# Output projection of a decoder layer: from a blocked product in 192 matmuls to Strassen's scheme in seven products

## The chip, the cores and the metric

The kernel runs on one core of a Trainium2 chip. The metric is the time of one execution on the device in microseconds (us). The kernel before was run three times: median 813.8 us, from 813.42 to 814.41. One further execution was taken by the hardware profiler; its own numbers stand in the table below.

## What is computed

One layer of a decoder on 512 tokens of width 1024, in float32. Two token mixers run in parallel: dilated window attention and a state-space scan. Each goes through its own projection (the branches), the two are merged by sigmoid gates, and the result is projected by `w_out`, added to the scaled input and normalized; a gated feed-forward part follows. What matters here is the middle:

```python
gates = jax.nn.sigmoid((gate_logits + b_gate[layer]).astype(jnp.float32))
mixed = gates[..., 0, :] * y_attn + gates[..., 1, :] * y_ssm
mix_out = mixed.astype(x.dtype) @ w_out[layer]            # (512 x 1024) @ (1024 x 1024)
h = layer_norm(DN_ALPHA * x + mix_out.astype(x.dtype), ln1_g[layer], ln1_b[layer])
ff = (jax.nn.silu(h @ w_ff_gate[layer]) * (h @ w_ff_up[layer])) @ w_ff_down[layer]
x = layer_norm(DN_ALPHA * h + ff.astype(h.dtype), ln2_g[layer], ln2_b[layer])
```

## The kernel before, in words

**Numbers in two parts.** Every float32 matrix that enters a matmul is split: `hi` is the value cast to the type fp32r (done by ACT, ScalarE), and `lo` is the rest, value minus `hi` (done by DVE, VectorE). A product is three matmuls, hi x hi, hi x lo and lo x hi (`mm3`, lines 205 to 208), all added up in one PSUM bank. In `add_remainder` (line 1509) the low part is made without DVE: ACT writes -hi into `lo`, and a transfer issued by POOL (GpSimd) adds the raw value from DRAM to it (line 1511). An adding transfer is a DMA with `accum_op=ALU.add`.

**Weights.** The class `Weights` hands out the weights in order. A unit of 1024 KB is loaded by SP (SyncE) into one of two `wraw` buffers and split in two halves into slots of hi and lo; `release()` gives back the oldest slot, and the next half is split into it at once. When the second half of a unit is split, `load()` issues the load of the unit after next. When the units are used up, functions listed in `w.jobs` and `w.loads` take their place: the feed-forward weights. `w.after` holds a postponed subtraction, which the next `flush()` emits. There are three slots at first and two more (`pb`) once the attention's tiles are freed (line 1429).

**Order of the work.** The schedule is written out by hand: on each engine the instructions run in the order of the program. A tile that takes the place of an older one waits until all uses of the older one are over. `home(n, ...)` names such a place of 8 KB per partition.

**Branches, lines 1394 to 1423.** Eight steps n = 0 to 7, each with 24 matmuls of 512 columns. From n = 4 on, the gated sums become the mixer's output `mx` (line 1416 hi, line 1421 lo), two of eight K-slices per step.

**Output projection, lines 1560 to 1636.** Four token tiles t of 128, two halves of 512 columns, eight K-slices, three matmuls each: 4 x 2 x 8 x 3 = 192 matmuls. The first half's four tiles are summed side by side while the units of `w_out` are split; the second half goes tile by tile. `wo_out` (line 1566) adds the scaled input from PSUM and takes the statistics of the normalization on DVE; `rstd` has one small operation on POOL; `normalize_shared` (line 1455) does half of a tile on DVE and half on ACT and POOL. `turn_h` (line 1573) transposes a normalized tile by eight PE transposes and splits it; `turn_lows` emits the subtractions on DVE.

**What stands around it.** The feed-forward product is already done by Strassen's scheme in pairs of blocks: `product(j, n)` is pair j, product n, 24 matmuls of 256 columns. Pair 0 needs sums of weight blocks: s5 from the block `early`, s6 and s3 and s7 from `early` and `ra[0]` (lines 1604, 1611, 1629, 1631). Its first products (0,1) and (0,2) use token tiles 0 and 1 only; tiles 2 and 3 are turned behind them. The weights (0,1), (0,2), (1,1), (1,2) are loaded by POOL as hi directly (line 1531), and their low parts come by adding transfers.

Of the kernel before, what the change touches and what calls it, by code (L numbers as in the profile page):

```python
# [16 lines left out]
P = 128  # L17
# [154 lines left out]
def emit(ctx, tc, i, out):  # L172
# [42 lines left out]
    def kslice(pair, k, cols=slice(None)):  # L215
        return pair[0][k // 4][:, k % 4, cols], pair[1][k // 4][:, k % 4, cols]
# [30 lines left out]
    w = Weights(nc, wp, split)  # L247
    out_homes = deque(("g0", 2, 6, 3))
    w.add(None, 8)
# [1142 lines left out]

    mx = act_pair("mix")
    for n in range(8):
        ws = w.views[N_BR + n]
        src = (gh_, gl_) if n < 4 else (merged["h"], merged["l"])
# [13 lines left out]
        for c, (ch, t0, t1) in enumerate(ts_):  # L1410
            if n < 4:
                stt(t1, t1, 1.0, bs[c], ALU.add, ALU.mult)
            else:
                stt(t0, t0, 1.0, bs[c], ALU.add, ALU.mult)
                tt(t0, t0, t1, ALU.add)
                act.mul(kslice(mx, ch)[0], t0, 0.5)
        flush()
        if n >= 4:
            for ch, t0, _ in ts_:
                hi, lo = kslice(mx, ch)  # L1420
                stt(lo, t0, 0.5, hi.bitcast(F32), ALU.mult, ALU.subtract)
        w.release()
# [46 lines left out]
    ht = []  # L1469
    early = home(7, "early")  # L1470
    sp.dma_start(early, i["w_gu"][1])
    s5 = home(8, "s5")[:, 0:1024]
    s6 = bt.tile([P, 1024], F32, tag="fth", name="s6", bufs=1)
# [25 lines left out]
    def load_dn(z, block, q):  # L1499
        dn[block, q] = z  # L1500
        sp.dma_start(z, i["w_dq"][block, q])

    w.loads[ff_first] = deque((lambda j=j: load_a(j)) for j in (0, 1))

# [21 lines left out]
    def prepare(j, n):  # L1526
# [9 lines left out]
        if j == 0 and n in (5, 6, 3, 7):  # L1536
            src = {5: s5, 6: s6, 3: s3, 7: s7}[n]
# [21 lines left out]

    def wo_mm(d, n, t):  # L1560
        ws = w.views[N_OUT + n]
        for k in range(2):
            kk = 2 * (n % 4) + k
            mm3(d, kslice(mx, kk, slice(128 * t, 128 * t + 128)), (ws[0][:, k, :], ws[1][:, k, :]), kk == 0, kk == KT - 1)

    def wo_out(d, t, e):
        cs = slice(512 * e, 512 * e + 512)
        stt(hn[t][:, cs], xn[t // 2][:, t % 2, cs], ALPHA, d, ALU.mult, ALU.add)
        dve.bn_stats(bst1[t][:, e, :], hn[t][:, cs])

    hturn = ring(4, 5, 6, 7)

# [21 lines left out]

    od = [bank(4 + t, f"wo0{t}") for t in range(NTT)]
    for n in range(4):
        for t in range(NTT):
            wo_mm(od[t], n, t)
        if n < 3:
            w.release()  # L1600
            if n < 2:
                w.split()
        if n == 2:
            tt(s5, early[:, 0:1024], early[:, 1024:2048], ALU.add)
    for t in range(NTT):
        wo_out(od[t], t, 0)
    od = [bank(t, f"wo1{t}") for t in range(NTT)]
    w.release()
    while w.free:
        w.split()  # L1610
    tt(s6, s5, ra[0][:, 0:1024], ALU.subtract)
    w.flush()
    mvs = [bt.tile([P, 4], F32, name=f"mva{t}", bufs=1) for t in range(NTT)]
    for t in range(NTT):
        for n in range(4, 8):
            wo_mm(od[t], n, t)
            if n == (None, None, 6, 5)[t]:
                turn_h(t - 2)
        if t == 3:
            turn_lows()  # L1620
            normalize_shared(hn[2], mvs[2], lnb)
        wo_out(od[t], t, 1)
        dve.bn_aggr(mvs[t][:, 0:2], bst1[t])
        rstd(mvs[t])
        turn_lows()
        if t < 2:
            normalize_shared(hn[t], mvs[t], lnb)
        if t == 0:
            tt(s3, ra[0][:, 1024:2048], s6, ALU.subtract)
        if t == 1:  # L1630
            tt(s7, ra[0][:, 0:1024], early[:, 0:1024], ALU.subtract)
            hp_ = tuple([home(h, f"h{n}{j}", F32R).rearrange("p (k t) -> p k t", k=4) for j, h in enumerate(hs)] for n, hs in (("h", (7, 8)), ("l", ("g1", 1))))
        if t in (0, 1):
            for _ in range(2):
                remainders.popleft()()
    normalize(hn[3], mvs[3], lnb)


# [10 lines left out]

    sums = home(6, "sums").rearrange("p (n c) -> p n c", n=2)  # L1650
    quad = home(3, "quad").rearrange("p (c e t) -> p c e t", c=4, e=2)
# [473 lines left out]
```

## Time and profile before

| | before |
|---|---|
| median of three runs | 813.8 us |
| profiled execution, its own time | 813.21 us |
| its span, first to last instruction | 811.4 us |
| mean granted TensorE clock | 0.995 |
| PE busy | 799.9 us (99%) |
| DVE busy | 669.8 us (83%) |
| ACT busy | 417.3 us (51%) |
| POOL busy | 88.5 us (11%) |
| DMA, all queues | 122.73 MB, mean 151 GB/s |

How to read the profile: times are microseconds from the span's start unless marked ns. PE is the matmul engine, PEld its weight loads; DVE is VectorE, ACT is ScalarE, POOL is GpSimd, SP is SyncE, which here only issues transfers. L1511 is line 1511 of the kernel. A line of a timeline gives start, duration, engine, line, operation, result <- operands, shape, how many were merged (x2), and in brackets how long the engine sat idle before and what it waited for. A group line gives minimum, median and maximum duration in ns, first and last start, and the shape. A waits line gives who waited for whom, the sum, the number of times and the longest. A windows line gives, for a stretch of time, the busy time and count of PE, PEld, DVE, ACT and POOL, then the granted clock, the busy share of the 16 DMA engines and GB/s moved. The chain of work that ended last is followed back from the last instruction.

### The profile page before, as it was taken

To read this page: it belongs to the slowest core of one execution; us is meant where nothing else is said; L and a number is where in the kernel's file an instruction comes from. 1 tells how busy PE (TensorE), PEld (TensorE's weight loads), DVE (VectorE), ACT (ScalarE), POOL (GpSimd) and SP (SyncE) were. 2 spreads that over 40 slices of the span, in tenths; PEclk is the share of its full clock that TensorE was granted. 3 is DMA by queue.
4 is the path that set the end of the run, shared out by engine and by line. 5 is a ranking of instruction groups with operands and counts; after the bars stand their busy time and mean duration, and the time that the engine had idled before them with its cause. 6 is when DMAs were issued, how large, how long until landed. Compare 5 with 4: busy or idle time off the path is not lost.

```text
span 811.4 us, 13836 instructions
## 1 busy us (share of the span) xinstructions
PE 799.9 (99%) x5584; PEld 720.1 (89%) x5584; DVE 669.8 (83%) x1066; ACT 417.3 (51%) x615; POOL 88.5 (11%) x110
## 2 busy tenths in 40 slices
PE   9999999999999999999999999999999999999995
PEld 7888888888999999988888899999999999888884
DVE  7987998979788799466796799887777789788986
ACT  5973222537575645874243466555555556554521
POOL 0000002230011333000000620000000000010105
PEclk9999999999999999999999999999999999999998
DMA  8753447895145654751728373622222324674544
GB/s 333 195 122 102 139 156 230 207 196 147 30 113 119 147 103 108 239 190 52 282 106 286 68 219 86 252 105 104 104 105 105 105 104 154 263 160 149 139 122 104
DMA packets 33488, 122.73 MB, mean 151 GB/s; under 512 B 7824, under 2 KB 12688, under 8 KB 23952
## 3 DMA queue, kind: packets, MB, share of 16 engines
q1 hardware_dynamic: 23808, 91.83, 33.0%
q0 software_dynamic: 7984, 28.32, 16.9%
q10 hardware_dynamic: 1632, 1.70, 0.6%
q8 instruction: 44, 0.72, 0.4%
q14 instruction: 20, 0.16, 0.1%
HBM read 105.84 MB, written 9.70 MB: 142 GB/s over the span
## 4 chain that ended last, share of the span: by engine, by line
PE 95%; DMA 2%; POOL 1%; DVE 1%; issue 0%; ACT 0%; DVEq 0%; POOLq 0%
PE qx L1261 7%; PE dnx L1872 6%; PE dnz L1872 4%; PE qz L1261 4%; PE pu L616 3%; PE pg L206 3%; PE vx L1217 3%; PE pg L207 3%; PE pg L208 3%; PE dny L1872 2%; DMA wlo<-in_w_gu 2%; PE s L840 2%; PE b L206 2%; PE b L207 2%; PE b L208 2%; PE qy L1261 2%
## 5 line engine op out<-in xcount | busy, mean ns | idle before, releaser
L1543 ACT CAST whi<-sums 128x1024 fp32r<-128x1024 f32 x40 | 42.0, 1051 | 61.3 <-DVE sums L344 61.3
L200 DVE TENSOR_TENSOR wlo<-raw,whi 128x1024 fp32r<-128x1024 f32 x40 | 48.8, 1223 | 16.4 <-ACT whi L199 16.4
L199 ACT CAST whi<-raw 128x1024 fp32r<-128x1024 f32 x40 | 41.7, 1048 | 17.1 <-PE pk L207 11.3
L344 DVE TENSOR_TENSOR wlo<-sums,whi 128x1024 fp32r<-128x1024 f32 x40 | 48.8, 1220 | 0.0
L1156 ACT CAST whi_q<-rq 128x1024 fp32r<-128x1024 f32 x28 | 29.3, 1052 | 35.7 <-DVE rq L344 25.1
L344 DVE TENSOR_TENSOR wlo_q<-rq,whi_q 128x1024 fp32r<-128x1024 f32 x28 | 34.2, 1221 | 15.8 <-ACT whi_q L1156 15.6
L1872 PE MATMUL dnx<-whi_d,pc 128*128 128x512 f32 (+1 forms) x128 | 38.2, 376 | 0.0
L853 ACT ACTIVATE un<-un,st 128x256 f32<-128x256 f32 (+1 forms) x64 | 30.9, 487 | 13.3 <-DVE st L851 13.3
L206 PE MATMUL pg<-x_hi,whi 128*128 128x512 f32 x96 | 37.6, 392 | 0.0
L778 POOL DMA_DIRECT2D kq<-qz x32 | 25.3, 1752 | 111.8 <-ACT un L865 70.9
L207 PE MATMUL pg<-x_lo,whi 128*128 128x512 f32 x96 | 37.4, 390 | 0.0
L208 PE MATMUL pg<-x_hi,wlo 128*128 128x512 f32 x96 | 37.4, 389 | 0.0
L968 ACT ACTIVATE gt<-pg,bgate 128x512 f32<-128x512 f32 x12 | 8.3, 690 | 41.8 <-PE pg L208 41.8
L1784 ACT CAST whi_d<-dn 128x1024 fp32r<-128x1024 f32 x16 | 16.9, 1056 | 23.0 <-DVE dn L344 11.1
L1872 PEld LDWEIGHTS dnx<-whi_d,pc 128*128 128x128 f32 x128 | 23.6, 188 | 4.4
L1794 POOL DMA_DIRECT2D whi_db<-in_w_dp x3 | 1.6, 547 | 228.8 <-PE dny L1872 225.1
L1872 PE MATMUL dnx<-wlo_d,pc 128*128 128x512 f32 (+1 forms) x64 | 24.1, 376 | 0.0
L1261 PE MATMUL qx<-x23h,whi_q 128*128 128x256 f32 x80 | 23.1, 289 | 0.0
L1261 PE MATMUL qz<-x_hi,whi_q 128*128 128x256 f32 x80 | 22.9, 287 | 0.0
L1261 PE MATMUL qz<-x_hi,wlo_q 128*128 128x256 f32 x80 | 22.6, 283 | 0.0
L1261 PE MATMUL qz<-x_lo,whi_q 128*128 128x256 f32 x80 | 22.6, 283 | 0.0
L1261 PE MATMUL qx<-x23h,wlo_q 128*128 128x256 f32 x80 | 22.6, 283 | 0.0
(894 smaller groups left out, 2627.9 us busy)
## 6 DMA issues: line engine op xcount, KB each, us to landing
raw<-in_w_in SPq DMA_DIRECT2D x12, 1024.0 KB, 5.4
ra<-in_w_gu SPq DMA_DIRECT2D x11, 1024.0 KB, 4.8
rb<-in_w_gu SPq DMA_DIRECT2D x10, 1024.0 KB, 4.9
rq<-in_w_quad SPq DMA_DIRECT2D x16, 512.0 KB, 4.4
dn<-in_w_dq SPq DMA_DIRECT2D x8, 1024.0 KB, 4.8
rv<-in_w_in SPq DMA_DIRECT2D x4, 1024.0 KB, 8.6
kq<-qz POOLq DMA_DIRECT2D x32, 128.0 KB, 5.9
raw<-in_w_br SPq DMA_DIRECT2D x4, 1024.0 KB, 5.0
```

Source lines behind the costliest of these rows:

```text
L199: act.copy(hi, src)
L200: dve.tensor_tensor(lo, src, hi.bitcast(F32), op=ALU.subtract)
L206: pe.matmul(dst, a[0], b[0], start=first, stop=False)
L207: pe.matmul(dst, a[0], b[1], start=False, stop=False)
L208: pe.matmul(dst, a[1], b[0], start=False, stop=last)
L344: eng.tensor_tensor(o, a, b, op=op)
L778: pool.dma_start(dst[32 * q : 32 * q + 32], z[32 * (q ^ 1) : 32 * (q ^ 1) + 32], accum_op=ALU.add)
L853: act.activation(pt, pt, AF.Exp, bias=mneg, scale=-1.0, accum_out=zsum)
L1156: act.copy(hi, src)
L1261: pe.matmul(d[:, 256 * e : 256 * e + 256], p_[:, e, k, :], q_[:, k, :], start=(first and e == k == m == 0), stop=(k == 3 and m == 2), skip ...
L1543: act.copy(hi, src)
L1872: pe.matmul(acc[key][0 if key == "v" else e][:, cs], p_, q_[:, cs], start=(key, e) not in begun, stop=(m == 2), skip_group_check=True)
```

## The change

The output projection is done by the Winograd form of Strassen's scheme on 2 x 2 blocks: tokens in halves of 256, K in halves of 512, columns in halves of 512. Seven products of 24 matmuls of 512 columns take the place of the 192. With A the mixer's output and B the weights:

- S1 = A21 + A22, S2 = S1 - A11, S3 = A11 - A21, S4 = A12 - S2, summed by DVE from the gated sums; the kernel holds -S4.
- T1 = B12 - B11 (held as its negative in `rt1`, loaded as `u`), T3 = B22 - B12 (`rt3`), T2 = T3 + B11 (`rt2`), T4 = T2 - B21 (held as its negative in `rt4`). ACT makes the negatives or copies, and adding transfers on POOL's queue add the other block from DRAM.
- Products 1: A11 B11, 2: A12 B21, 5: S1 T1, 6: S2 T2, 3: S4 B22, 4: A22 T4, 7: S3 T3, in this order; product 7's and 4's token tiles take turns at the end, with the transposes of h between them.

The blocks of products 1, 2 and 3 are pure weights: POOL loads hi directly, ACT writes the negative, POOL's transfer adds the raw block. Product 7's low parts come by adding transfers from `rt3` in SBUF. For products 5, 6 and 4 DVE subtracts as before. The first transfers are issued inside the branches, from n = 1 on. The sum s5 is made by an adding transfer into `early`, and the low parts of the feed-forward weights (0,5) and (0,3) by adding transfers too. `early` and `ra[0]`, `ra[1]` are loaded later, into the buffers of `rt1`, `rt3` and `early`. The evictions have a first part with the scaled input (`out_first`) and added parts (`out_add`).

```diff
@@ units: w_out is no longer among them
-    for un in range(2):
-        w.add(i["w_out"][un], 2)
-    for un in range(2, 4):
-        w.add(i["w_out"][un], 2, lambda name, dt: home(out_homes.popleft(), name, dt))
@@ branches
+    def load_b12():
+        wo_raw["u"] = wp.tile([P, 2048], F32, tag="wraw", name="wo_t1", bufs=2)
+        sp.dma_start(wo_raw["u"], i["w_out"][2])
...
+    def pure(m, block, h, l):
+        hi, lo = home(h, f"wo{m}h", F32R), home(l, f"wo{m}l", F32R)
...
+        pool.dma_start(hi, i["w_out"][block])
+        def rest():
+            act.mul(lo, hi.bitcast(F32), -1.0)
+            pool.dma_start(lo, i["w_out"][block], accum_op=ALU.add)
+        return rest
+    def sums_of_b12(n):
+        u = wo_raw.get("u")
+        if n == 4:
+            act.mul(u, u, -1.0)
+        elif n == 5:
+            act.copy(wo_raw["t3"], u)
+            pool.dma_start(u, i["w_out"][0], accum_op=ALU.add)
+            pool.dma_start(wo_raw["t3"], i["w_out"][3], accum_op=ALU.add)
     for n in range(8):
+        if n == 1:
+            later_rest[5] = pure(1, 0, 6, 3)
+        if n == 4:
+            later_rest[5.5] = pure(2, 1, "g0", 2)
+        if n == 5:
+            later_rest[5]()
+        sums_of_b12(n)
+        if n == 6:
+            later_rest[5.5]()
...
-                act.mul(kslice(mx, ch)[0], t0, 0.5)
+                cs = slice(0, 512 if ch >= 4 else 256)
+                act.mul(kslice(mx, ch, cs)[0], t0[:, cs], 0.5)
@@ feed-forward weights of pair 0
+        if j == 0 and n in (5, 3):
+            low_by_transfer(hi, lo, src)
+            return
@@ the stage
+    def out_product(m, e, ks=range(4)):
+        d = obank[okey[m]][e]
+        for k in ks:
+            a = [z[:, k, 128 * e : 128 * e + 128] for z in mix_part(m)]
+            b = [z[:, k % 2, :] for z in wo_ops[m][k // 2]]
+            for q, (p_, q_) in enumerate(((0, 0), (0, 1), (1, 0))):
+                pe.matmul(d, a[p_], b[q_], start=(m in (1, 2, 4, 5) and k == q == 0), stop=(k == 3 and q == 2), skip_group_check=True)
...
+    def low_by_transfer(hi, lo, raw):
+        act.mul(lo, hi.bitcast(F32), -1.0)
+        pool.dma_start(lo, raw, accum_op=ALU.add)
+    tt(s1_, g0_[:, :, h2_], g1_[:, :, h2_], ALU.add)
+    rt2 = home(1, "wo_t2")
+    wo_ops[5] = [slot_ops(5, 0)]
+    act.copy(wo_ops[5][0][0], half_of(rt1, 0))
+    low(5, 0, rt1)
+    act.copy(rt2, rt3)
...
+    for u in range(2):
+        pool.dma_start(wo_ops[3][u][0], half_of(i["w_out"][3], u))
+    pool.dma_start(rt2, i["w_out"][0], accum_op=ALU.add)
+    act.mul(mix_part(5)[0], s1_, 0.5)
+    mix_low(5, s1_)
...
+    sp.dma_start(early, i["w_gu"][1])
+    for e in range(2):
+        out_product(1, e)
+    for t in range(2):
+        out_first(t, 0, obank["x"][t])
+    act.mul(mix_part(6)[0], s2_, 0.5)
+    mix_low(6, s2_)
+    for u in range(2):
+        hi, lo = wo_ops[3][u]
+        act.mul(lo, hi.bitcast(F32), -1.0)
+        pool.dma_start(lo, half_of(i["w_out"][3], u), accum_op=ALU.add)
...
+    for e in range(2):
+        out_product(2, e)
...
+    for u in range(2):
+        act.copy(wo_ops[6][u][0], half_of(rt2, u))
+        low(6, u, rt2)
+    rt4 = home("g1", "wo_t4")
+    act.mul(rt4, rt2, -1.0)
+    pool.dma_start(rt4, i["w_out"][1], accum_op=ALU.add)
+    for t in range(2):
+        out_add(t, 0, obank["y"][t])
+        stats(t, 0)
+    slot3 = slot_ops(7, 0)
+    act.copy(slot3[0], half_of(rt3, 0))
+    low_by_transfer(*slot3, half_of(rt3, 0))
...
+    for e in range(2):
+        out_product(5, e)
+    for _ in range(2):
+        w.release()
+    pool.dma_start(early[:, 1024:2048], i["w_gu"][1][:, 0:1024], accum_op=ALU.add)
+    for t in range(2):
+        out_first(2 + t, 1, obank["z"][t], ALU.subtract)
...
+    for e in range(2):
+        out_product(6, e)
...
+    for u in range(2):
+        act.copy(wo_ops[4][u][0], half_of(rt4, u))
+        low(4, u, rt4)
+    act.copy(wo_ops[7][1][0], half_of(rt3, 1))
+    low_by_transfer(*wo_ops[7][1], half_of(rt3, 1))
+    load_a(0)
+    for _ in range(2):
+        remainders.popleft()()
...
+    for t in range(2):
+        out_product(3, t)
+        out_add(t, 1, obank["z"][t], ALU.subtract)
+        stats(t, 1)
+        moments(t)
...
+        normalize_shared(hn[t], mvs[t], lnb)
+    tt(s6, early[:, 1024:2048], ra[0][:, 0:1024], ALU.subtract)
...
+    out_product(4, 0)
+    out_first(2, 0, obank["y"][0])
+    out_product(7, 0, range(3))
+    turn_h(0)
+    out_product(7, 0, range(3, 4))
...
+    out_product(4, 1)
+    turn_h(1)
...
+    out_product(7, 1)
+    out_add(3, 0, obank["x"][1])
+    stats(3, 0)
+    out_add(3, 1, obank["x"][1])
+    stats(3, 1)
+    moments(3)
     normalize(hn[3], mvs[3], lnb)
+    w.release()
+    tt(s7, ra[0][:, 0:1024], early[:, 0:1024], ALU.subtract)
+    load_a(1)
@@ after product(0, 2) and the turns of tiles 2 and 3
+    tt(s3, ra[0][:, 1024:2048], s6, ALU.subtract)
+    w.release()
```

More of the change, by code (lines that the diff above doesn't have):

```diff
@@ L1393, in emit, with place_t3, by_k @@
     mx = act_pair("mix")
-    for n in range(8):
+    wo_raw, wo_ops = {}, {}
+    def load_b12():
+        wo_raw["u"] = wp.tile([P, 2048], F32, tag="wraw", name="wo_t1", bufs=2)
+        sp.dma_start(wo_raw["u"], i["w_out"][2])
+    def place_t3():
+        wo_raw["t3"] = wp.tile([P, 2048], F32, tag="wraw", name="wo_t3", bufs=2)
+    w.loads[2 * len(w.units)] = deque((load_b12, place_t3))
+    def by_k(z):
+        return z.rearrange("p (k c) -> p k c", c=512)
+    def pure(m, block, h, l):
+        hi, lo = home(h, f"wo{m}h", F32R), home(l, f"wo{m}l", F32R)
+        wo_ops[m] = [(by_k(hi)[:, 2 * u : 2 * u + 2], by_k(lo)[:, 2 * u : 2 * u + 2]) for u in range(2)]
+        pool.dma_start(hi, i["w_out"][block])
[11 more added lines that the diff above has]
+            pool.dma_start(wo_raw["t3"], i["w_out"][3], accum_op=ALU.add)
+    later_rest = {}
+    for n in range(8):
+        if n == 1:
[7 more added lines that the diff above has]
+            later_rest[5.5]()
         ws = w.views[N_BR + n]
@@ L1536, in prepare @@
         if j == 0 and n in (5, 6, 3, 7):
-            src = {5: s5, 6: s6, 3: s3, 7: s7}[n]
+            src = {5: early[:, 1024:2048], 6: s6, 3: s3, 7: s7}[n]
         else:
@@ L1571, in emit, with out_first, out_add, stats @@
-    hturn = ring(4, 5, 6, 7)
+    xres = [xn[t // 2][:, t % 2] for t in range(NTT)]
+    def out_first(t, e, d, op=ALU.add):
+        stt(hn[t][:, halves[e]], xres[t][:, halves[e]], ALPHA, d, ALU.mult, op)
+    def out_add(t, e, d, op=ALU.add):
+        tt(hn[t][:, halves[e]], hn[t][:, halves[e]], d, op)
+    def stats(t, e):
+        dve.bn_stats(bst1[t][:, e, :], hn[t][:, halves[e]])
+    mixed = {1: (0, 0), 6: (0, 0), 5: (0, 1), 7: (0, 1), 2: (1, 0), 3: (1, 0), 4: (1, 1)}
+    obank = {k: [bank(b + e, f"wo{k}{e}") for e in range(2)] for k, b in (("x", 4), ("z", 6), ("y", 0))}
@@ new lines, in slot_ops, with half_of, mix_low, low @@
+    def slot_ops(m, u):
+        hi, lo = w.take_slot(f"wo{m}{u}")
+        return by_k(hi), by_k(lo)
+    def half_of(z, u):
+        return by_k(z[:, 1024 * u : 1024 * u + 1024])
+    def mix_low(m, src):
+        hi, lo = mix_part(m)
+        stt(lo, src, 0.5, hi.bitcast(F32), ALU.mult, ALU.subtract)
+    def low(m, u, raw):
+        hi, lo = wo_ops[m][u]
+        tt(lo, half_of(raw, u), hi.bitcast(F32), ALU.subtract)
+    g0_, g1_ = gts[0], gts[1]
+    free_ = gts[2].rearrange("p q t -> p (q t)")
@@ new lines, in emit @@
+    s1_, s2_ = (free_[:, 1024 * e : 1024 * e + 1024].rearrange("p (k t) -> p k t", k=4) for e in range(2))
+    h1_, h2_ = slice(0, 256), slice(256, 512)
+    rt1, rt3 = wo_raw["u"], wo_raw["t3"]
+    def low_by_transfer(hi, lo, raw):
[6 more added lines that the diff above has]
+    low(5, 0, rt1)
@@ new lines, in emit @@
+    act.copy(rt2, rt3)
+    wo_ops[5].append(slot_ops(5, 1))
+    wo_ops[3] = [slot_ops(3, u) for u in range(2)]
+    for u in range(2):
[3 more added lines that the diff above has]
+    mix_low(5, s1_)
+    act.copy(wo_ops[5][1][0], half_of(rt1, 1))
+    tt(s2_, s1_, g0_[:, :, h1_], ALU.subtract)
+    low(5, 1, rt1)
+    early = wp.tile([P, 2048], F32, tag="wraw", name="early", bufs=2)
@@ new lines, in emit @@
+    for e in range(2):
+        out_product(2, e)
+    hi6, lo6 = home(6, "wo6h", F32R), home(3, "wo6l", F32R)
+    wo_ops[6] = [(by_k(hi6)[:, 2 * u : 2 * u + 2], by_k(lo6)[:, 2 * u : 2 * u + 2]) for u in range(2)]
+    for u in range(2):
[7 more added lines that the diff above has]
+        stats(t, 0)
@@ L1593, in turn_lows @@
             tt(*lows.pop(0), ALU.subtract)
[L1595 to L1610, printed above, removed]
@@ L1623, in emit, with moments @@
+    def moments(t):
         dve.bn_aggr(mvs[t][:, 0:2], bst1[t])
         rstd(mvs[t])
[L1625 to L1629, printed above, removed]
+    for t in range(2):
+        out_product(3, t)
+        out_add(t, 1, obank["z"][t], ALU.subtract)
+        stats(t, 1)
+        moments(t)
         if t == 1:
-            tt(s7, ra[0][:, 0:1024], early[:, 0:1024], ALU.subtract)
-            hp_ = tuple([home(h, f"h{n}{j}", F32R).rearrange("p (k t) -> p k t", k=4) for j, h in enumerate(hs)] for n, hs in (("h", (7, 8)), ("l", ("g1", 1))))
@@ L1636, in emit @@
+    out_add(2, 0, obank["x"][0])
+    stats(2, 0)
+    out_add(2, 1, obank["x"][0])
+    stats(2, 1)
+    moments(2)
+    turn_lows()
+    out_product(4, 1)
+    turn_h(1)
+    for _ in range(2):
+        remainders.popleft()()
+    out_first(3, 0, obank["y"][1])
+    turn_lows()
+    normalize_shared(hn[2], mvs[2], lnb)
+    out_product(7, 1)
[4 more added lines that the diff above has]
+    moments(3)
     normalize(hn[3], mvs[3], lnb)
+    w.release()
```

54 lines of the change are left out of this document (23 added, 31 removed).

## The prediction, made blind

> **What bounds the kernel now.** I read the page first (busy times, chain that ended last), then PE's waits, then the groups of the stage that the change rewrites.
>
> ```profile
> span 811.4 us, 13836 instructions
> PE 799.9 (99%) x5584; PEld 720.1 (89%) x5584; DVE 669.8 (83%) x1066; ACT 417.3 (51%) x615; POOL 88.5 (11%) x110
> PE 95%; DMA 2%; POOL 1%; DVE 1%; issue 0%; ACT 0%; DVEq 0%; POOLq 0%
> PE warm_b L288 <- DVE warm L284: 1.1, 1, 1.1
> PE fs1y L1672 <- DMA wlo<-in_w_gu: 0.4, 1, 0.4
> ```
>
> PE is busy for 99% of the span and is 95% of the chain. In the whole run it waits twice, the second time for 0.4 us, and that wait is for an adding transfer (the low part of a feed-forward weight). So a matmul taken away is worth its full pitch, and any new wait of PE costs its full length: there is no slack to pay it from.
>
> ```profile
> 400.45 0.39 PE L206 MATMUL b<-ath,whi 128*128 128x512 f32 x1
> L206 PE MATMUL wo<-whi,mix_hi x32: 389/389/389, 422.2 to 443.3; 128*128 128x512 f32 x32
> L208 PE MATMUL wo<-w,mix_lo x32: 389/389/397, 444.4 to 467.3; 128*128 128x512 f32 x32
> 481.57 2.88 PE fs0z L1672 x24
> ```
>
> Branch n=4 starts at 400.45 and the output projection at 422.2: four branches of 24 matmuls in 21.75 us, a pitch of 0.2266 us. (The 389 ns of a single matmul overlap its neighbours.) The 192 matmuls of the projection, with sixteen transposes among them, end at 467.5. The first product that needs everything behind the stage, fs0z, product (0,5), starts at 481.57; I measure the change by where that start moves.
>
> **What goes.** Seven products of 24 matmuls are 168 in place of 192: 24 x 0.2266 = **5.4 us** less PE work. Transposes and feed-forward products are the same. This is all the change can win, besides the 0.4 us wait, which I take out and reckon anew.
>
> **What the operands now cost.** Before, DVE and ACT made the weights' low parts from plain loads. Now POOL's queue carries adding transfers: 1 MB each for wo1l, the two sums u (rt1) and t3 (rt3), wo2l, rt2, rt4, 1 MB in two for product 3's low parts, 0.5 MB each for both low parts of product 7 and for the sum `early`. The rows for such a transfer are the group of `add_remainder`'s line (L1511) with its landings, three windows of 2 us, and two of the DMA issues; the window at 394 is for plain loads:
>
> ```profile
> L1511 POOL DMA_DIRECT2D wlo<-in_w_gu x2: 922/1052/1181, 457.0 to 457.6; - x2
> DMA to landing us min/median/max: 5.5/6.6/7.7
> 458.00:460.00 2.00, 2.00 (x14) 1.76 (x13) 0.55 (x2) 0.35 (x1) 1.42 (x2) 1.00 0.67 70
> 460.00:462.00 2.00, 2.00 (x10) 1.64 (x10) 2.00 (x3) 2.00 (x3) 1.45 (x1) 1.00 1.05 207
> 462.00:464.00 2.00, 2.00 (x11) 1.59 (x10) 1.77 (x5) 2.00 (x5) 1.92 (x3) 1.00 1.06 207
> w<-in_w_gu POOLq DMA_DIRECT2D x1, 512.0 KB, 5.3
> 394.00:398.00 4.00, 4.00 (x20) 3.30 (x19) 3.92 (x6) 1.05 (x1) 0.00 (x0) 1.00 0.98 408
> raw<-in_w_out SPq DMA_DIRECT2D x4, 1024.0 KB, 4.8
> ```
>
> The last two columns of a window are the DMA engines' busy share and GB/s. Two adding transfers of 512 KB issued 0.6 us apart land at 462.5 and 465.3: one behind the other, not together. While only they run, the engines are full (1.05) at 207 GB/s, where plain loads fill them at 408. So 1 MB (1.049 million bytes) takes 5.07 us added and 2.57 plain. One alone of 512 KB lands 5.3 us after issue, of which 2.53 is moving and 2.77 fixed. No transfer here has 1 MB in one issue with adding; bounds are the plain rate (2.57) and the 5.6 that the two landings give (2.8 for half); I take 5.1, nearest to the windows.
>
> The Trainium skill ("DMA: Bandwidth & Descriptors", section "Anatomy of one DMA — SWDGE (gpsimd) path") fits a GpSimd-issued transfer as 2.0 us and bytes over 436 GB/s, which would make 1 MB move in 2.4 us, adding or not. The windows above speak against it for adding ones, at 207 GB/s; the time by the page is that of the first rival below.
>
> **When the first four can be issued.** They hang on ACT.
>
> ```profile
> 397.21 25.20 SPq L121 DMA_DIRECT2D raw<-in_w_out  x3
> 408.72 1.04 ACT L199 CAST whi<-raw 128x1024 fp32r<-128x1024 f32 x1
> 425.28 1.99 ACT L199 CAST whi<-raw 128x1024 fp32r<-128x1024 f32 x2
> 426.35 2.36 DVE L200 TENSOR_TENSOR wlo<-raw,whi 128x1024 fp32r<-128x1024 f32 x2 [0.25 <-ACT whi L199]
> ```
>
> The block for u is loaded at 397.21, where the first block of w_out was, and negated by 404.5. ACT does wo1l's negative behind branch n=4's last weight cast (408.72 and 1.0 long); 2048 columns are about 1.95 us by the pair at 425.28, so wo1l's transfer is issued at about 411.5, u's and t3's behind ACT's copy at 413.4 and 414.3, wo2l's behind its negative at 416. All four are issued before the first has landed, so they run in line: the last lands at 411.5 + 2.8 + 4 x 5.1 = **434.7**.
>
> **Product 1** (422.2 to 427.65) has its operands; wo1l lands at 419.4. **Product 2** wants wo2l at its second matmul, 427.9: it waits **6.6 us** and ends at 440. That alone is more than the 5.4 gained. Product 5 has u (424.5) and its sums in time: to 445.4.
>
> **Product 6** needs rt2. Its copy waits for t3 (429.5), so it is issued at 431.5, behind wo2l (to 434.4) and the 1 MB plain load of product 3's high parts (2.6), then moves 5.1 us beside the plain `early` load (2.6 more, SP's queue): it lands at about 444.7. ACT's cast (1.05) and DVE's subtract (1.2) follow: **1.6 us** of wait. DVE stands in order behind that subtract, with the evictions of products 2 and 5 queued behind it, so product 3 gets its bank late: **1.0 us**.
>
> **Product 4** needs rt4: negated at 448.5, moved behind product 3's low parts (to 449.8), landed at 455.8, cast and subtracted by 458: just in time. But ACT makes product 7's second negative behind these casts, at 459.7, and on POOL's queue that transfer stands behind 0.5 MB (first low part), 1 MB plain (two feed-forward weights) and 0.5 MB (`early`): it lands at 466.1. Product 7's third k-step wants it at 462.8: **3.3 us**.
>
> ```profile
> 451.61 0.94 POOL L1439 TENSOR_TENSOR mva<-mva,epsb 128x1 f32<-128x1 f32 x1 [12.09 <-DVE mva L336]
> 453.67 2.02 POOL L1465 TENSOR_TENSOR hn<-hn,lnb 128x512 f32<-128x512 f32 x1 [1.13 <-ACT hn L1464]
> 441.21 0.68 DVE L341 SCALAR_TENSOR_TENSOR hn<-xn,wo 128x512 f32<-128x512 f32 x1
> 480.36 1.21 PE fs1y L1672 x8
> ```
>
> POOL normalizes behind those issues (0.94 for the power, 1.3 to 2.0 per half): the two turns wait **1.3 us** in sum. Then `load_a(0)` reuses rt3's buffer, so SP holds it until 466.1; it lands at about 473 beside two more adding transfers. DVE stands at the subtract for s6, which needs it, with some twelve instructions of 0.3 to 1.2 us (evictions like that at 441.21, statistics, low parts of h) queued behind. The low parts of h come at 481, where the first feed-forward product, begun at 475.9, wants them after 8 matmuls (0.96 us; eight take 1.21 with the last one's tail): **4.4 us**. The last token tile now has two additions and two statistics behind its last matmul instead of one each: **1.1 us** before its turn, and the sums for product (0,5) another **1.1**, because DVE comes to them late.
>
> The loads of the second feed-forward pair (`ra`, `rb`) follow on SP only when product (0,5)'s low part has landed, near 491; they land by 500, and product (1,5) wants them made up at 509: in time.
>
> DVE's added work (about 7 us: 14 sums and low parts of 1.14 and 8 evictions of 0.61, against 8 low parts, s5's sum and half of the mix's low parts and two feed-forward ones gone) and ACT's 21 us (six operations of 1.95 and 18 casts of 0.95, against 8) fit beside the transfers, since both engines idle for several us at each landing; without that cover they would be late by those sums.
>
> **Sum.** 6.6 + 1.6 + 1.0 + 3.3 + 1.3 + 4.4 + 1.1 + 1.1 = 20.4 of waits, less 5.4 and 0.4: **+14.6 us**. The profiled execution took 813.2 us (span 811.4), so 827.8; the median before is 813.8, which lies 0.6 above it. I predict **828.0 us**, 1.7% slower.
>
> **Rivals.**
>
> *Transfers hidden* (faster). If 1 MB adds at the plain rate, wo2l lands at 411.5 + 2.8 + 4 x 2.57 = 424.6, before product 2. The point is 411.5 + 2.8 + 4y = 427.9, y = 3.4 us per MB. Then only the tail's waits stay, about 3.5 us in all (turns 1.3, first feed-forward product 0.4, last tile and sums 2): 813.2 - 5.4 - 0.4 + 3.5 = 811, down to 808 if those go too. For it: no row has an adding transfer of this size. Against it: the engines' share is 1.05 at 207 GB/s, so they are full, and the size of a row changes nothing in that. **0.10.**
>
> *Only part of the waits.* Adding at about 4.2 us per MB, or DVE's and SP's late work reaching PE less than I reckon: product 2 waits 2.5, product 7 0.8, the first feed-forward product 3, others 3 to 5: 815 to 822. **0.17.**
>
> *Slow matmuls after a wait.*
>
> ```profile
> 4.63 0.63 PE L616 MATMUL pu<-x_lo,wuh 128*128 128x256 f32 x2
> 5.06 0.52 PE L616 MATMUL pu<-x_hi,wul 128*128 128x256 f32 x2
> 5.66 0.40 PE L616 MATMUL pu<-x_lo,wuh 128*128 128x256 f32 x2
> 5.90 0.40 PE L616 MATMUL pu<-x_hi,wul 128*128 128x256 f32 x2
> ```
>
> Early in the span a pair of matmuls takes 0.43 us (4.63 to 5.06), a moment later 0.24 (5.66 to 5.90); late data may have a share in that. If PE falls back to the slow pace after waits of 6.6, 3.3 and 4.4 us, each costs some 1.5 us; half is swallowed by the next wait, for a landing that doesn't move: 2 to 4 us more, 830 to 832. The Trainium skill ("TensorE: Matmul & The Clock Gate", "Part 1: The HAM clock gate (the "warmup" mystery)") has such a rule: half clock after an idle window of about 3.4 us. No wait of before after the start is long enough to show it. **0.15.**
>
> *No change*, gain and waits in balance within 0.2% (1.6 us, about what measurement can tell): **0.03.** The forecast itself, 823 to 830, has **0.55**.
>
> Faster 0.10, same 0.03, slower 0.55 + 0.17 + 0.15 = 0.87. The range takes in the partial case and the slow-pace case, with 5.6 us per MB at the top (+4 us by then, on seven transfers whose landings bind in part): 815 to 835.
>
> **What would show it.** PE's waits name the low part of product 2's weights at about 428, 5 to 7 us long; then `wo4`/`w` low parts and `hl` of DVE near 463 and 477. DMA windows of 414 to 434 read about 205 GB/s at full share. SP's first `ra` load goes out after 464 instead of 431. The forecast is wrong if those windows read over 300 GB/s, or if PE's waits between 422 and 500 sum to under 6 us.

## The result and the profile after

The changed kernel takes **836.9 us** (median of four runs, 836.49 to 837.03) against 814.1 for the kernel before, measured beside it: ratio **1.028** (95% interval 1.0265 to 1.0291). The direction is the forecast's, the time is 8.9 us above its 828.0 and 1.9 above its range. The profiled execution took 836.83 us.

Three lines of the page of the changed kernel (span; busy time of each engine; the chain that ended last, by engine), and the list of what PE waited for (sum, times, longest):

```profile
span 834.9 us, 13854 instructions
PE 803.6 (96%) x5560; PEld 721.9 (86%) x5560; DVE 676.3 (81%) x1077; ACT 437.1 (52%) x631; POOL 100.6 (12%) x127
PE 87%; DMA 5%; issue 3%; DVE 2%; ACT 1%; POOL 1%; DVEq 0%; POOLq 0%; SPq 0%; ACTq 0%
```

```profile
PE woy L1625 <- DMA wo2l<-in_w_out: 7.3, 1, 7.3
PE fs0x L1830 <- DVE hl L339: 4.4, 1, 4.4
PE wox L1625 <- DMA wo7u<-wo_t: 4.4, 1, 4.4
PE fs0z L1830 <- ACT hh L1892: 2.3, 1, 2.3
PE fs0z L1830 <- DMA wlo<-snaps: 0.3, 1, 0.3
```

24 matmuls are gone (5584 to 5560), and yet PE is busy for 3.7 us more. The waits are where the forecast put the large ones: product 2's low part (7.3 us), product 7's second low part (4.4), the first feed-forward product (4.4), and ahead of (0,5) (2.3). They make 18.7 us where there was 0.4. That PE's busy time grew in spite of fewer matmuls has a reason that the windows show (columns: stretch, its length, busy time and count of PE, PEld, DVE, ACT, POOL, granted clock, DMA share, GB/s):

```profile
428.00:430.00 2.00, 0.00 (x0) 0.00 (x0) 0.06 (x1) 0.00 (x0) 0.00 (x0) 1.00 1.03 213
430.00:432.00 2.00, 0.00 (x0) 0.00 (x0) 0.00 (x0) 1.64 (x1) 0.00 (x0) 0.68 1.06 221
436.00:438.00 2.00, 2.00 (x7) 1.54 (x6) 2.00 (x4) 1.73 (x2) 0.00 (x0) 0.50 1.19 256
442.00:444.00 2.00, 2.00 (x11) 1.64 (x10) 0.00 (x0) 0.00 (x0) 0.00 (x0) 1.00 0.98 320
```

In 428 to 432 PE stands still while the DMA engines are full at 213 to 221 GB/s: adding transfers, close to the 207 that the forecast took from two windows of the old trace. When the matmuls resume at 435.24, they run at half the granted clock until about 441: 6 or 7 in 2 us in place of 9 to 11. The same happens behind the other three waits; at (0,5) the clock falls only after the matmuls have resumed:

```profile
500.94 1.22 PE L1830 MATMUL fs0z<-hh,whi 128*128 128x256 f32 x8 [2.26 <-ACT hh L1892]
500.00:502.00 2.00, 1.06 (x8) 1.01 (x8) 2.00 (x2) 1.78 (x2) 0.86 (x1) 1.00 1.00 401
502.00:504.00 2.00, 1.90 (x10) 1.74 (x9) 2.00 (x3) 1.10 (x2) 0.00 (x0) 0.60 0.91 279
```

From the rows, matmuls ran at a granted 0.50 for 5.8 us behind product 2's wait, 3.3 behind product 7's, 4.7 and 3.4 behind the two in the feed-forward part: 17.2 us, so about **8.6 us of matmul time lost**. This is close to the 8.9 us by which the forecast missed, and was my first explanation. The experiments say otherwise.

The forecast's timetable of landings, against the trace:

| what | forecast | landed |
|---|---|---|
| wo1l | 419.4 | 421.1 |
| u | 424.5 | 425.4 |
| t3 | 429.5 | 430.3 |
| wo2l | 434.7 | 435.2 |
| rt2 | 444.7 | 444.7 |
| rt4 | 455.8 | 456.8 |
| product 7's second low part | 466.1 | 468.4 |
| `ra[0]` | 473 | 476.4 |

### The profile page after: what moved, and what is told of

Its sections match the earlier page's. It is cut to its first block, busy times and chain, and to the rows that moved or that the text cites. A ratio compares the mean times of both kernels' runs of the same rounds, so it can differ in the third digit from the quotient of the medians.

```text
span 834.9 us, 13854 instructions
## 1 busy us (share of the span) xinstructions
PE 803.6 (96%) x5560; PEld 721.9 (86%) x5560; DVE 676.3 (81%) x1077; ACT 437.1 (52%) x631; POOL 100.6 (12%) x127
## 4 chain that ended last, share of the span: by engine, by line
PE 87%; DMA 5%; issue 3%; DVE 2%; ACT 1%; POOL 1%; DVEq 0%; POOLq 0%; SPq 0%; ACTq 0%
PE qx L1256 7%; PE dnx L2031 6%; PE dnz L2031 4%; PE qz L1256 4%; PE pu L611 3%; PE pg L206 3%; PE vx L1212 3%; PE pg L207 3%; PE pg L208 3%; PE dny L2031 2%; PE s L835 2%; PE qy L1256 2%; PE o L869 2%; PE t L858 2%; DMA wo_t<-in_w_out 1%
## 5 line engine op out<-in xcount | busy, mean ns | idle before, releaser
L200 DVE TENSOR_TENSOR wlo<-raw,whi 128x1024 fp32r<-128x1024 f32 x36 | 43.8, 1220 | 16.2 <-ACT whi L199 16.2
L199 ACT CAST whi<-raw 128x1024 fp32r<-128x1024 f32 x36 | 37.6, 1048 | 17.4 <-PE pk L207 11.3
```

Of the source, the lines that this page charges most:

```text
L200: dve.tensor_tensor(lo, src, hi.bitcast(F32), op=ALU.subtract)
```

## The experiments

The letters in the expectations of e1 to e4 name other theories in each run, as the text there says. From e5 on the same two are set against each other: A, that the lost matmul time counts; B, that a chain of transfers and queues sets the time and PE's pace inside it does not.

### Idle matmuls in the waits (e1_busy, e5_busy2)

`keep_busy` issues the given number of matmuls into a PSUM bank that nobody reads. The comments behind # in this cut and in that of e4_s6 are notes for the reader.

```diff
+    keep_busy("busy2", 30, 2, spare, wo_ops[1][0][0][:, 0, :])      # ahead of product 2
     for e in range(2):
         out_product(2, e)
...
+    keep_busy("busy7", 17, 2, spare, wo_ops[7][0][0][:, 0, :])      # inside product 7
+    keep_busy("busyf", 32, 3, wh[:, 0, 0, :], mh[:, 0, :])          # inside the first product
+    keep_busy("busy5", 14, 5, ops[0, 5][0][:, 0, 0, :], hp_[0][0][:, 0, 0:256])   # ahead of (0,5)
```

> The changed kernel, with idle matmuls put where PE waits longest: 30 of 512 columns ahead of product 2, 17 inside product 7's first token tile, 32 of 256 columns inside the first feed-forward product, 14 of 256 ahead of product (0,5). They write a spare bank that nobody reads; every result stays. Theory A (waits cost twice: their length, and half clock for some us after each of 4 us or more): the granted clock stays 1.0 through the stage, product 2 ends near 440.5 instead of 443; the small waits before products 6 and 3 that the slow matmuls had covered (about 1 us each) come back; 829 to 833 us. Theory B (the half clock is covered by the next landing, so it costs nothing): 836 to 837, as before the edit. If the added matmuls themselves cost: above 838.

> The kernel with idle matmuls in TensorE's waits once more, for a profile that can be read. Theory A (the half granted clock behind each wait, some 8.6 us, is what the forecast lacked): its earlier time of 838 must come from idle matmuls that push real ones back, so that the real matmuls of the products start later than in the changed kernel. Theory B (from product 2's wait to the first feed-forward product a chain of transfers sets the time: rt2's adding 432.6 to 444.7, w7's low 461.2 to 468.4, ra[0]'s load 468.6 to 476.4): granted clock near 1.00 all through, ra[0]'s load issued again at 468 to 470 although TensorE is at full clock, and the product waits longer by about what the matmuls gained; 836 to 839 us.

Measured in e1_busy: 837.1 to 839.1 us in three executions; the fourth, which was the profiled one, took 2078.7 us for a reason that the record does not show, so there is no trace to read. In e5_busy2, the same kernel: 836.2 us (ratio 1.0275, 1.0257 to 1.0294), with a mean granted clock of 0.996 against 0.981. So the clock was kept and the time hardly moved. Rows of e5_busy2, PE's and SP's timelines:

```profile
429.43 6.96 PE L1685 MATMUL busy<-wo1h,mix_hi 128*128 128x512 f32 x30
436.86 0.50 PE L1625 MATMUL woy<-wo2l,mix_hi 128*128 128x512 f32 x1 [0.24 <-DMA wo2l<-in_w_out]
448.18 0.50 PE L1625 MATMUL wox<-wo6h,mix_hi 128*128 128x512 f32 x1 [0.37 <-ACT wo6h L1694]
449.43 0.50 PE L1625 MATMUL wox<-wo6l,mix_hi 128*128 128x512 f32 x1 [0.76 <-DVE wo6l L339]
455.82 0.47 PE L1625 MATMUL woz<-whi_wo,mix_hi 128*128 128x512 f32 x1 [0.88 <-issue]
470.36 26.47 SPq L1524 DMA_DIRECT2D ra<-in_w_gu  x2
```

Product 2 ran at full pace and was through earlier, and PE then waited at product 6 (0.37 + 0.76 us) and at product 3 (0.88), where it had not waited before: the 1.6 and 1.0 us that the forecast had put there and the trace of the changed kernel lacked. The idle matmuls did not push the real ones back: PE still waited 0.24 us for wo2l behind them. `ra[0]` was issued at 470.36, 46.4 us after product 1's start at 423.99; in the changed kernel it was 468.56 - 422.14 = 46.4 as well. From product 1's start to the product fs2y it took 111.5 us against 113.1. So of 8.6 us of lost matmul time **1.6** reached the end by the traces; by the medians it is 0.7 in this run and nothing in the first.

### More work on PE (e8_extra)

```diff
+    for _ in range(15):
+        pe.matmul(extra, spare, wo_ops[5][0][0][:, 0, :], start=True, stop=True)
     for e in range(2):
         out_product(5, e)
```

> 15 more matmuls of 512 columns (3.4 us at full clock, 4 to 5 at the lower one) on TensorE ahead of product 5, with results that nothing uses. Theory B (TensorE is not on the path between product 2's wait and product 7's): the waits of 4.4 us at product 7 takes them up, 836 to 838 us. Theory A (every slow or added microsecond of matmuls counts): 839.5 to 842 us.

Measured: 837.9 us (1.0289, 1.0272 to 1.0306), 1.0 over the changed kernel. PE's waits in that run:

```profile
PE fs0x L1834 <- DVE hl L339: 3.8, 1, 3.8
PE fs0z L1834 <- DMA wlo<-snaps: 2.7, 1, 2.7
PE wox L1625 <- DMA wo7u<-wo_t: 2.3, 1, 2.3
```

The wait at product 7 shrank from 4.4 to 2.3 and took in most of the 3.4 us of added work; `ra[0]` was issued 46.8 us after product 1's start, 0.3 later than before. What its trace grew by lies mostly behind (0,5), where the wait for (0,3)'s low part grew from 0.3 to 2.7. Two kernels that change PE's pace between 435 and 468 in opposite directions leave the time nearly alone: that lost matmul time counts in full (A) is refuted, and B is borne out for this stretch.

### The adding rate (e2_plain)

```diff
-            pool.dma_start(lo, i["w_out"][block], accum_op=ALU.add)
+            pool.dma_start(lo, i["w_out"][block])
```

So with every adding transfer that the change brought: the same bytes land in the same order as plain transfers, and the additions are left out of the computation.

> The changed kernel with each of its own adding transfers (wo1l, u, t3, wo2l, rt2, product 3's and 7's low parts, rt4, early, low parts of (0,5) and (0,3)) turned into a plain one of the same bytes, queue, place and waits; the additions are left out, so sums and low parts hold other values. Theory A (the rate of adding, about 5 us per MB against 2.6 plain, makes the landings late): PE's waits for wo2l and product 7's low part go, and with them their slow clock; the wait for h's low parts shrinks below 2 us, since ra[0] is loaded sooner; 811 to 816 us. Theory C (the issue order on ACT and POOL makes them late, whatever the rate): waits of 4 us or more stay, 826 us or more.

Measured: 820.8 us (1.0081, 1.0063 to 1.01): 16 us less than the changed kernel, but 5 above the top of what was expected of the adding rate alone. Adding is the larger part of the loss, not all. One window, and two rows of PE and VectorE:

```profile
418.00:422.00 4.00, 4.00 (x19) 3.30 (x18) 2.56 (x5) 1.13 (x2) 0.00 (x0) 1.00 1.02 406
462.84 1.22 DVE L339 TENSOR_TENSOR s<-early,ra 128x1024 f32<-128x1024 f32 x1 [4.83 <-DMA ra<-in_w_gu]
470.39 2.08 PE L1830 MATMUL fs0x<-hl,whi 128*128 128x256 f32 x8 [4.43 <-DVE hl L339]
```

The same transfers fill the engines at 406 GB/s where adding ones reached 213 to 221, and the waits at products 2 and 7 are gone. But the wait of 4.4 us at the first feed-forward product stands unchanged, at an earlier time, where the expectation had less than 2 us. VectorE still stood 4.8 us for `ra[0]`, whose load, itself plain in both kernels, was issued at 452.6 and took 10.1 us to land. So this wait did not go with the adding rate; it hangs on the place of s6 in VectorE's queue, which e4_s6 changes.

### wo1l and wo2l earlier (e3_first)

```diff
-        if n == 5:
-            later_rest[5]()
         sums_of_b12(n)
-        if n == 6:
-            later_rest[5.5]()
+        if n == 4:
+            later_rest[5]()
+            later_rest[5.5]()
```

> The changed kernel with both negatives and adding transfers of the pure low parts of products 1 and 2 moved ahead, into branch n=4, so that wo2l is second in POOL's line and not fourth. Theory A (the sum of bytes to be added is the limit): product 2 no longer waits, but u and t3 stand behind it, t3 lands at most 1.5 us sooner, rt2 near 443, so a wait of 5 to 7 us stands ahead of product 6 in its place, with its slow clock: 833 to 837 us. Theory D (a bad order alone, with time to spare elsewhere): 826 to 830.

Measured: 835.9 us (1.0268, 1.0245 to 1.029). Product 2's wait is gone, and that at product 7 is 3.5 us in place of 4.4. New ones stand at products 5, 6, 3 and 4, six in all and 5.9 us in sum, the largest at product 5; the expectation had put all of it at product 6. PE's waits, among others:

```profile
PE wox L1624 <- DMA wo7u<-wo_t: 3.5, 1, 3.5
PE woz L1624 <- ACT mix_hi L1662: 2.4, 1, 2.4
PE woz L1624 <- issue: 0.8, 1, 0.8
```

rt2's transfer went out 12.7 us after product 1's start instead of 10.4, behind the two that had been moved ahead of it. The range expected of a limited supply of adding transfers, 833 to 837, was met: their order decided which product waits, and moved the time by 1.0 us.

### VectorE no longer stands at s6 (e4_s6)

```diff
-    tt(s6, early[:, 1024:2048], ra[0][:, 0:1024], ALU.subtract)     # ahead of product 4
...
     out_first(3, 0, obank["y"][1])
     turn_lows()
+    tt(s6, early[:, 1024:2048], ra[0][:, 0:1024], ALU.subtract)
```

> The changed kernel with one DVE instruction moved: s6 = s5 - ra[0] goes behind the low parts of h's first two token tiles instead of ahead of product 4's eviction, so DVE doesn't stand at ra[0]'s landing with everything queued behind it. Theory A: the 4.4 us wait in the first feed-forward product goes and its slow clock (2.3) with it, the last token tile is normalized sooner, and part of the waits at product (0,5) (2.3 and 1.7 of slow clock) goes: 826 to 831 us. If DVE has no room and the wait only turns up at product (0,6) or (0,3): 834 to 837.

Measured: 833.0 us (1.023, 1.0211 to 1.0248), 3.9 less, but 2 above what was expected. The wait of 4.4 us at the first feed-forward product is gone and its slow matmuls (2.3 us) with it: 6.7 us of PE, of which 3.9 reached the end. The waits at (0,5) and (0,3) did not go: 1.6 and 0.7 us are left of them.

### Product 7's second low part by VectorE (e6_sub7, e7_sub7_s6, e11_snap)

```diff
     act.copy(wo_ops[7][1][0], half_of(rt3, 1))
-    low_by_transfer(*wo_ops[7][1], half_of(rt3, 1))
+    low(7, 1, rt3)
```

> The second low part of product 7 made by a VectorE subtraction (1.18 us) in place of ScalarE's negative and the adding transfer (issue 461.2, landing 468.4). Theory B: ra[0]'s buffer is t3's, so its load is issued near 462 in place of 468.6 and lands near 470; the wait of 4.4 us at product 7 goes, that at the first feed-forward product stays between 2 and 5 us, and the time is 829 to 832 us. Theory A (clock): one wait of 4.4 us and its slow matmuls (1.7 us) go, 830 to 832, but ra[0]'s load would not move with it. A third one (ra[0]'s landing is set by the transfers' supply, not by the buffer): load issued early, landing near 476 as before, 835 to 837.

> The same, and the subtraction s6 behind h's low parts. Theory B: both waits go, VectorE's queue from the end of product 7's first tile to (0,5)'s operands is the limit, and that starts some 5 us earlier than with s6 moved alone (832.96): 826 to 829 us. If the two edits remove the same wait: 830 to 832.

Measured: 832.2 us (1.022, 1.0205 to 1.0235), 4.7 less than the changed kernel; with s6 moved as well 833.4 (1.0241, 1.0221 to 1.0261). SP's row of the first:

```profile
462.27 31.49 SPq L1524 DMA_DIRECT2D ra<-in_w_gu  x2
```

`ra[0]` is issued 6.3 us earlier: its buffer is t3's, and the adding transfer of product 7 had been the last reader of t3. This is the link of the chain that ties product 7 to the feed-forward part. The time alone would not have told B from A, which expected 830 to 832; the issue of `ra[0]` does. Against B's expectation the wait at the first feed-forward product went as well, and waits of 3.9 and 1.8 us stood at the turns instead. The two edits together gave no more than the first alone, 1.4 us above the upper of the two ranges expected. In both runs a wait had grown at the end of the stage, `fs0z <- DMA wlo<-snaps`, 2.1 and 3.7 us: the adding transfer for product (0,3)'s low part, 11.3 and 12.9 us from issue to landing. So that one went to VectorE too:

```diff
-        if j == 0 and n in (5, 3):
+        if j == 0 and n == 5:
```

> The changed kernel with product 7's second and product (0,3)'s low part subtracted by VectorE. The wait for the low part from snaps (2.1 us in the run with the first of the two edits) goes; VectorE's queue ahead of (0,5)'s operands is 1.2 us longer: 830.5 to 832.5 us, against 832.15.

This run has product 7's second low part by VectorE too, and s6 in its old place, so it differs from e6_sub7 by this edit alone. Measured: 829.2 us (1.0189, 1.0174 to 1.0204), 2.9 less than e6_sub7 and below what was expected: the wait is gone, and nothing came in its place.

### Fewer adding transfers, and the order of products (e9_plain, e10_all, e12_order, e13_order2)

rt2 and rt4 are loaded plainly and completed by VectorE, and product 7's second low part is subtracted as in e6_sub7; in e9_plain and e10_all, rt4's block, loaded before product 2, also serves product 2's low part. e10_all has s6 moved and (0,3)'s low part by VectorE as well.

```diff
+        if m == 2:
+            wo_raw["t4"] = home("g1", "wo_t4")
+            sp.dma_start(wo_raw["t4"], i["w_out"][block])
         def rest():
+            if m == 2:
+                tt(lo, wo_raw["t4"], hi.bitcast(F32), ALU.subtract)
+                return
...
-    act.copy(rt2, rt3)
-    pool.dma_start(rt2, i["w_out"][0], accum_op=ALU.add)
+    sp.dma_start(rt2, i["w_out"][0])
+    tt(rt2, rt2, rt3, ALU.add)
...
-    act.mul(rt4, rt2, -1.0)
-    pool.dma_start(rt4, i["w_out"][1], accum_op=ALU.add)
+    rt4 = wo_raw["t4"]
+    tt(rt4, rt4, rt2, ALU.subtract)
```

> The same result with fewer adding transfers: product 2's low part, rt2 and rt4 from plain loads and VectorE additions and subtractions (2.3 us each; block 1 loaded once serves product 2's low part and rt4), product 7's second low part as in the run before. Theory B (supply of adding transfers, then the chain over ra[0]'s buffer to VectorE's queue): wait at product 2 below 1 us, none at products 6 and 7, ra[0] issued before 458, and what is left is VectorE's queue between product 3's evictions and product (0,5): 817 to 825 us. If VectorE has no room for the 5.7 us that this adds: 826 to 832.

> The same, with s6 behind h's low parts and product (0,3)'s low part subtracted by VectorE instead of added by a transfer. Theory B: the wait for that low part (2 to 4 us in the two runs before) goes as well, 814 to 821 us. If VectorE's queue is the limit there already: within 1 us of the run without these two edits.

Measured: 839.1 us (1.0309, 1.0294 to 1.0324) and 837.4 (1.0286, 1.0269 to 1.0303): far above the 817 to 825 and 814 to 821 expected. Two rows of the first show my error:

```profile
422.89 0.33 SPq L1410 DMA_DIRECT2D wo_t<-in_w_out  x1
434.38 2.29 DVE L339 TENSOR_TENSOR wo2l<-wo_t,wo2h 128x2048 fp32r<-128x2048 f32 x1 [19.38 <-DMA wo_t<-in_w_out]
```

The place that I gave the block is in use until 422.9, and the block lands only at 434.4. The subtraction stood in VectorE's order in branch n = 6, and the engine stood there for 19.4 us with the mixer's last steps queued behind it. It says nothing on B; it repeats at another place what s6 does.

The next one starts from the 829.2 us kernel, leaves product 2's low part as it was, computes product 5 ahead of product 2, and keeps the plain rt2 and rt4.

> The last kernel (two low parts by VectorE), and besides: product 5 ahead of product 2, so that wo2l's adding transfer has 5.4 us more, and rt2 and rt4 from plain loads with VectorE's addition and subtraction (no adding transfer behind wo2l and ahead of product 3's low parts). Theory B: the wait of 6.9 us at product 2 falls to 1 to 3 us and its slow matmuls with it; products 6, 4 and 7 wait for nothing; what remains is VectorE's queue at the first turn and ahead of (0,5): 819 to 825 us against 829.2. If VectorE's queue behind the products, and not the wait at product 2, sets the time: 827 to 830. Faster than 814 by neither.

Measured: 837.2 us (1.0283, 1.0266 to 1.03). Product 3's operand of the mix is written into product 2's place; with the order turned round it was written first, so product 2 multiplied another operand and waited 15.8 us for it: no answer to the question. e13_order2 puts this right (the plain rt2 as above, product 3's negatives behind product 6's copies):

```diff
     for e in range(2):
-        out_product(2, e)
+        out_product(5, e)
...
-    act.mul(rt4, rt2, -1.0)
-    pool.dma_start(rt4, i["w_out"][1], accum_op=ALU.add)
+    sp.dma_start(rt4, i["w_out"][1])
+    tt(rt4, rt4, rt2, ALU.subtract)
...
     for e in range(2):
-        out_product(5, e)
+        out_product(2, e)
+    act.mul(mix_part(3)[0], g1_[:, :, h1_], 0.5)
+    mix_low(3, g1_[:, :, h1_])
```

> The order tried in the run before, put right: product 3's operand of the mix made behind product 2, which reads the same buffer, and the negatives for product 3's low parts behind product 6's copies on ScalarE. Theory B as there: wait at product 2 of 1 to 3 us in place of 6.9; the transfers ahead of product 3's low parts (four of 1 MB adding, 20 us, and four plain, 10 us, from 414 on) end near 445, its low parts near 451, so product 3 waits some 2 us: 821 to 826 us against 829.2. If the supply moves the whole wait of product 2 to product 3: 828 to 831.

Measured: **824.7 us** (1.013, 1.0114 to 1.0147), as expected, 12.2 less than the changed kernel with the same seven products. PE's larger waits:

```profile
PE woy L1625 <- DMA wo2l<-in_w_out: 3.1, 1, 3.1
PE hb L1737 <- POOL hn L1507: 2.2, 1, 2.2
PE fs0z L1830 <- ACT hh L1892: 1.7, 1, 1.7
PE hb L1737 <- DVE hn L336: 1.5, 2, 1.1
```

It is still some 10.5 us slower than the kernel before, which took 814.2 beside it. With 5.4 us to gain, some 10 us of waits are left (the four above and 1.6 us in three small ones); the remaining 6 us, slow matmuls behind waits and the end of the span among them, were not taken apart.

### What sets the end of the stage (e15_stats, e16_stats13), and the end of the span (e14_before)

In the changed kernel and in the last variant, the statistics of token tiles 2 and 3 are taken from 64 of 512 columns, which shortens VectorE's queue alone (what is normalized with them differs).

```diff
-        dve.bn_stats(bst1[t][:, e, :], hn[t][:, halves[e]])
+        dve.bn_stats(bst1[t][:, e, :], hn[t][:, 512 * e : 512 * e + (512 if t < 2 else 64)])
```

> The changed kernel, with the statistics of token tiles 2 and 3 taken from 64 of 512 columns (what is normalized with them differs); VectorE's four instructions of 0.69 us become short, some 2.2 us less in its queue between ra[0]'s landing and product (0,5). Theory B (from ra[0]'s landing on VectorE's queue sets the time): 834 to 835.5 us against 836.9. If TensorE or ScalarE sets it there: within 0.6 us of 836.9.

> The same on the version with the corrected order of products (824.74). Theory B: 822 to 823.5 us. If the waits for transfers and TensorE itself set its time: within 0.6 us of 824.7.

Measured: 835.4 us (1.026, 1.0244 to 1.0275), 1.5 less; and 824.7 (1.013, 1.0112 to 1.0147), no difference. That VectorE's queue behind `ra[0]`'s landing sets the time is borne out for the changed kernel and refuted for the variant. The chain of the variant's run that ended last (start, length, what) names another engine:

```profile
463.70 1.27 POOL hn L1506
...
468.42 1.99 POOL hn L1506
470.48 1.29 POOL hn L1507
472.27 0.94 POOL mva L1480
...
475.84 0.93 POOL wlo L1548
476.79 0.90 POOL wlo L1548
477.68 1.33 POOL hn L1506
```

There POOL's queue leads: normalizations of 1.3 to 2.0 us, the small powers, and between them the issues of adding transfers, 0.9 us each. This is read from one chain; no run shortens POOL's queue.

> The kernel of before once more, for the end of its trace: from the start of the last group of matmuls (dnv) to the end of the span it took 13.1 us in the first profile, and 14.5 in that of the changed kernel and of every variant. If that is a matter of the kernel, 13.1 again; if of the single execution, another value; either way 0.0 to 1.4 us of the difference.

The second profile of the kernel before (815.0 us in a single run) has 13.1 us from dnv to the end of the span, as the first; the changed kernel has 14.5 and its variants 14.1 to 14.6. So 1.4 us belong to the changed program. The last output transfer lands 2.1 us after its issue in both kernels, so the 1.4 us come behind the last landing, where the trace shows no work; their cause stays open.

## Why the prediction was right, and where it was wrong

**Right:** that the gain is 24 x 0.2266 us and that there is no slack to pay a wait from; that the time grows; that adding transfers run one behind the other at half the plain rate (213 to 221 GB/s in the windows; 16 us of the time go when they become plain). The Trainium skill's fit for GpSimd-issued transfers ("DMA: Bandwidth & Descriptors", "Anatomy of one DMA — SWDGE (gpsimd) path"), by which we estimate 2.4 us of moving per MB, does not agree with any of these windows of adding transfers; the forecast's rival with the plain rate put wo2l's landing at 424.6, and it came at 435.2. Product 2's wait was put at 6.6 us and was 7.3; product 7's at 3.3 and was 4.4; the first feed-forward product's at 4.4 and was 4.4; the last tile's turn and (0,5), 1.1 + 1.1, came as one wait of 2.3 at (0,5). `ra[0]` went out behind 464, at 468.6, as the forecast said it would show. That wo2l's landing came out within 0.5 us is in part luck: the first of the four adding transfers landed 9.5 us after its issue where the forecast has 7.9, and the others followed 4.3, 4.9 and 4.9 us apart where it has 5.1.

**Wrong in form, not in size:** products 6 and 3 (1.6 + 1.0) and the turns (1.3) did not wait in the changed kernel, because the slow matmuls ahead of them used that time up. With the clock kept, the waits at products 6 and 3 came back (0.37 + 0.76 and 0.88), and those at the turns, too (1.2 + 0.8). So the rival "slow matmuls after a wait" was no rival: it comes together with the forecast. Its price of 2 to 4 us net was nearer to the measured 1.6 than the raw 8.6. The Trainium skill ("TensorE: Matmul & The Clock Gate", "Part 1: The HAM clock gate (the "warmup" mystery)") gives half clock after an idle window of about 3.4 us. Behind product 1 the trace agrees in size: PE is idle from 428, and the granted clock falls within 430 to 432. At (0,5) it does not: PE stood for only 2.26 us there, and the clock fell all the same.

**The step that failed** is the one on `load_a(0)`: "SP holds it until 466.1; it lands at about 473". The link was right (t3's buffer, proved by the subtraction in its place: issue at 462.27), but its term was mis-sized: product 7's low part was issued at 461.2 and took 7.2 us, not 6.4 from 459.7, and `ra[0]` took 7.9, not 6.9. That makes 1.5 + 0.8 + 1.0 = 3.3 us. These rows of the changed kernel's chain show it, and what follows:

```profile
461.20 7.22 DMA wo7u<-wo_t
468.56 7.87 DMA ra<-in_w_gu
476.56 1.23 DVE s L339
...
484.10 3.78 PE fs0x L1830 x16
...
500.01 11.00 DMA wlo<-snaps
511.05 1.22 PE fs0z L1830 x8
```

The sum also stopped too early, at the first start of fs0z, and it put at nothing the one adding transfer that binds behind it: (0,3)'s low part, `wlo<-snaps`, which took 11.0 us, and for which PE waits 0.3 us at 511. By the forecast that start would be 14.6 us late; by the timelines it went from 481.4 to 500.9, 19.5 us, and fs2y from 513.1 to 535.2, 22.1:

| where | us |
|---|---|
| `ra[0]` lands at 476.4, not 473 | 3.4 |
| from there to fs0z's first matmul | 1.5 |
| behind it, to fs2y: 22.1 - 19.5 | 2.6 |
| from fs2y to the end of the span, and outside it | 1.5 |
| sum: 836.8 - 827.8 | 9.0 |

The first row lies on the chain that ended last, and e6_sub7, in which `ra[0]` was issued 6.3 us earlier, gained 4.7 before POOL's normalizations and (0,3)'s transfer took the lead; that all of the 3.4 us reached the end is read from the chain and not shown by a run. Of the second row 1.0 us is the slow pace: with the clock kept, fs0z started 23.5 us behind the landing in place of 24.5. The third row is mostly (0,3)'s transfer, and hardly the slow pace. From fs0z's start to fs2y's it took 31.7 us before and 34.3 in the changed kernel; with the clock kept it took 34.0, as the wait for that low part grew from 0.3 to 1.5; with the low part by VectorE it took 32.1, against 34.6 in e6_sub7. Rows of PE's timeline in e11_snap and e6_sub7:

```profile
495.94 1.21 PE L1830 MATMUL fs0z<-hh,whi 128*128 128x256 f32 x8 [1.68 <-ACT hh L1892]
528.05 1.12 PE L1830 MATMUL fs2y<-hh,whi 128*128 128x256 f32 x8
496.72 1.22 PE L1830 MATMUL fs0z<-hh,whi 128*128 128x256 f32 x8 [1.70 <-ACT hh L1892]
531.30 1.12 PE L1830 MATMUL fs2y<-hh,whi 128*128 128x256 f32 x8
```

The last row's cause is open. The range ended at 835 because its top took in only a slower adding rate and the rival of 830 to 832, and nothing for links behind fs0z.

**Chances.** "Slower" had 0.87. Of the rivals, hidden transfers needed 3.4 us per MB; the landings were 4.3 to 4.9 us apart, near the forecast's 5.1.

## What to carry to other kernels

Where PE is the chain, look for what a new wait is tied to before adding up what PE loses: time lost ahead of a landing that doesn't move is swallowed, here 7 of 8.6 us, while taking the last reader off one buffer brought a load forward by 6.3 us and the end by 4.7. An adding transfer took twice as long as a plain one here (about 213 GB/s against 406) and kept its source in use until it landed: before using one, ask who gets the source's buffer next. And carry a sum of shifts on to the point where the old rhythm returns, not to the first product behind the stage.

## What the runs showed of the hardware

- Adding transfers: 213 to 221 GB/s at a full DMA share, where the same transfers without adding reach 406. One of 512 KB beside plain loads took 11 to 13 us from issue to landing (`wlo<-snaps`).
- The granted clock fell 2 to 4 us after PE's work stopped, once (within 502 to 504) when it had already resumed, and PE then worked for 3.3 to 5.8 us at half of it; idle matmuls with unused results kept its mean at 0.996.
- 1.4 us at the end of the span, behind the last landing, that came and went with the program and not with the execution (13.1 us from dnv twice before; 14.5 in the changed kernel, 14.1 to 14.6 in its variants).
